# Four wait times of a hand-made schedule raised, and one barrier moved behind a projection, in a hybrid SSD and chunk-MLP encoder block

## Chip, cores and metric

The kernel runs on one core of a Trainium2 chip. The metric is the device time of one execution in microseconds, as the median of several. A core has a matrix engine (TensorE, PE in the rows; PEld are its weight loads), a vector engine (VectorE, DVE), a scalar engine (ScalarE, ACT), GpSimd (POOL), and SyncE (SP), which here issues nearly all DMA transfers. Each engine works through its own list of instructions in the order in which the program issued them, and waits there for semaphores.

## What is computed

One layer of a streaming encoder, for one prompt of 1024 rows and eight sample streams of 16 rows. Both go through the same weights, so the kernel treats them as nine tiles of 128 rows (tile 8 is the samples). In the reference, cut:

```python
h = rms_norm(x, norm_g[0]) * (1 + sc1) + sh1
z, xbc, dt_raw, uv = split(h @ w_in)
xbc_act = silu(causal_conv(xbc))              # 4 taps
dt = softplus(dt_raw + dt_bias)
y = ssd_scan(xs, dt, A, Bm, Cm, h0)           # chunked scan: gates, y_diag, y_off, state
y_ssd = rms_norm((y + d_skip * xh) * silu(z), ssd_norm_g)
u, v = split(gelu(uv)); v = layer_norm(v, v_ln_g, v_ln_b)
y_cmlp = u * (tril(w_s) @ v + b_s)
m = concatenate([y_ssd, y_cmlp]) @ w_out
x = x + g1 * rms_norm(m, norm_g[1])
h = rms_norm(x, norm_g[2]) * (1 + sc2) + sh2  # the second norm
x = x + g2 * rms_norm(square(relu(h @ w_ff1)) @ w_ff2, norm_g[3])
```

## The kernel before

The nine tiles are three groups of three (tiles 0 to 2, 3 to 5, 6 to 8). Every product is done in split fp32: an operand is a high part `hi` and a low part `lo`, and three matmuls hi·hi, hi·lo and lo·hi add up in one PSUM bank. ACT rounds the high part, DVE or GpSimd subtracts it to get the low part. Low parts of weights that a later group needs are stored to DRAM (`kl`) and loaded again (`wl<-kl`).

The program is written out by a scheduler of generators. A main generator issues the projections: `m_in(g)` for the input projection of group g (eight conv blocks `xbc`, z in two halves `pz0` and `pz1`, four `pu`, v in two halves `pv0` and `pv1`), then `m_out(g)` for the output projection (`wo`). After each block it yields an estimate of its time, and `tick` adds that to a build-time clock and steps eight lanes of side tasks. A side task issues a few instructions, yields a number from the table `WAIT` (`wait("dA", g)` takes `dA0`, `dA1`, `dA2` for the three groups), and is stepped again once the clock has passed that many ns. So the table decides behind how much projection work a side task's next matmul stands in the PE queue. Nothing of it is a wait on the chip. `finish(tasks)` ticks the clock in steps of 500 ns until the tasks are done, with no projection work issued meanwhile.

The side tasks that the change touches:

- `prep1_task(g)` makes `hT[g]`, the normed and modulated input of group g, transposed and split. Two rows of x give `ss`, GpSimd makes `r` from it, then comes `wait("prep1_tr", g)`. For each tile the matmul `pr` (L506) spreads `r`, DVE multiplies (L507), ACT modulates (L427; on DVE, L433 and L434, for tile 8), and a split writes `hT` (L238, L241). The first split of a group waits until the task given as `after` is done. For group 2 that is `ssd_tasks[1]`, since `hT[2]` lies in the memory of `gA[1]`, which that scan reads.
- `ssd_gates(g)` makes softplus on DVE (`ab`, `e` on ACT, `z`, `q`, `dt`, `dA`, L764 to L790), then `wait("dA", g)`, then the sums `pa` (L797, L798) on PE, the copy `nac` (L805) on DVE, `wait("pn", g)`, the transpose `pn` (L813), and from it `hl`, `lt` and `rr`.
- `ssd_tile(g, tl)` is the scan of a tile: `px`, `pbn` and `par` on PE, then `L` on ACT and DVE (L892), then `wait("yd", g)` and the products `yd`, `yo`, `su` on PE. All tiles of all groups run one after the other in lane A, and `tail_task` (z gate, norm, transposes `yT`) follows each in lane D.
- `prep2_first` makes the second norm of group 0, whose transposes `pt` (L252) wait for `M` (L456, L470). It runs behind `out_task(0)`.

`yT[2][0]` takes the memory of `M[0]`, so `ssd_task(2)` may begin only when `prep2_first` (`p0`) is done.

Of the kernel before, what the change touches and what calls it, by code (L numbers as in the profile page):

```python
# [41 lines left out]
def shape_constants():  # L42
# [14 lines left out]


WAIT = dict(
    L=12100, L0=3200, L1=0, L2=400, dA=28300, dA0=2400, dA1=2800, dA2=3200, evac=4100, gs1=4100, h0=4100, ln=5900,  # L60
    ln0=7300, ln1=9100, ln2=10000, lnr=5600, lnr0=2800, lnr1=600, lnr2=2000, modB=3000, modC=7600, mod_gate=2000,
    mod_load=8200, mod_mt=2100, next8=0, nexttile=6700, nexttile0=800, nexttile1=2400, nexttile2=1900, pn=20800,
    pn0=1900, pn1=0, pn2=3800, prep1_load=17400, prep1_load1=1700, prep1_load2=3200, prep1_next=13800,
    prep1_next1=4400, prep1_next2=1000, prep1_norm=11500, prep1_norm1=3300, prep1_norm2=800, prep1_split=40000,
    prep1_split1=400, prep1_split2=1000, prep1_stat=6500, prep1_stat1=1000, prep1_stat2=0, prep1_tr=5600,
    prep1_tr1=0, prep1_tr2=3500, prep2_load=1700, prep2_load0=200, prep2_load1=1500, prep2_load2=3600,
    prep2_next=3200, prep2_next0=2800, prep2_next1=2500, prep2_next2=5000, prep2_norm=6200, prep2_norm0=4000,
    prep2_norm1=3500, prep2_norm2=5000, prep2_split=1700, prep2_split0=1200, prep2_split1=800, prep2_split2=1500,
    prep2_stat=9600, prep2_stat0=1500, prep2_stat1=2500, prep2_stat2=4500, rr=11700, rr0=800, rr1=13000, rr2=400,
    set_load=10000, set_pcc=0, set_pw=2900, sp=13000, sp0=800, sp1=500, sp2=1900, sp_mid=22500, sp_mid0=9600,  # L70
    sp_mid1=0, sp_mid2=1400, sz=20900, sz0=1300, sz1=800, sz2=0, x1=14700, x10=2500, x11=7200, x12=4700, xr=29300,
    xr0=3000, xr1=2600, xr2=2700, yT=45700, yT0=2500, yT1=5600, yT2=2800, yc=23700, yc0=15400, yc1=16900,
    yc2=9500, yd=400, yd0=4500, yd1=6000, yd2=4900, yo8=2500, yr=11700, yr0=200, yr1=0, yr2=1100)
ENG = dict(p1hi=1, p2hi=0, ychi=0, yc=1, xdt=1, xw=1, xnD=1, L0=0, L1=0, sp=0, vg=0, vb=1, xr=1, S=0, rr=0, sz=1)
LO_POOL = {0, 1, 6, 7, 8, 9, 10, 11, 12, 13, 14, 15, 16, 17, 18, 19, 20, 21, 22, 24, 25, 26, 27, 28, 31, 32, 33, 35, 36, 39, 40, 41, 42, 43, 44, 46, 52, 53, 54, 55, 56, 60, 63, 64, 66, 68, 70, 72, 73, 77, 79, 80, 83, 85, 87, 89, 90, 91, 92, 93, 94, 95, 96, 97, 98, 100, 102, 103}
LOADS = [
# [41 lines left out]
def tile_block(ctx, tc, io, out):  # L118
# [59 lines left out]
    mod_tasks, out_tasks, flags = {}, {0: [], 1: [], 2: []}, {}  # L178
# [12 lines left out]
    def finish(*tasks):  # L191
        for t in tasks:
            while not t.done:
                tick(500.0)
# [382 lines left out]
    def m_proj_a(g, n, name, evac):  # L577
        accs = [None] * GT
        for half in range(2):
            wh, wl = w_next()  # L580
            for tl in range(GT):
                if half == 0:
                    accs[tl] = mmt(f"{name}_{tl}")
                xs = hT[g][half][:, :, :, P * tl:P * tl + P]
                o = accs[tl][:, 0:n]
                for k in range(4):
                    pe.matmul(o, xs[:, k, 0], wh[:, k, :], start=half == 0 and k == 0, stop=False)
                    pe.matmul(o, xs[:, k, 1], wh[:, k, :], start=False, stop=False)
                for k in range(4):
                    pe.matmul(o, xs[:, k, 0], wl[:, k, :], start=False, stop=half == 1 and k == 3)  # L590
                flush()
                if half == 1:
                    evac(tl, accs[tl])
                if tl == 0:
                    w_low()
                yield 4 * T_A
# [102 lines left out]
    def m_in(g, ct0=0):  # L699
# [8 lines left out]
        def ev_z(half):  # L708
            def f(tl, a):
                if half == 0:  # L710
                    dve.tensor_tensor(dtx[g][:, tl, :], a[:, 0:8], dtb, op=ALU.add)
                a = a[:, 8:264] if half == 0 else a[:, 0:256]
                th = gt(f"zt{g}{tl}{half}")
                act.activation(th, a, AF.Tanh, scale=0.5)
                dve.scalar_tensor_tensor(sz[g][:, tl, 256 * half:256 * half + 256], th, 1.0, a, op0=ALU.add, op1=ALU.mult)
                zdone[g] = tl + GT * half
            return f
# [2 lines left out]
            yield from m_proj_b(g, f"xbc{g}_{ct}", lambda a, ct=ct: xbc_evac(g, ct, a))  # L720
        if g > 0:
            finish(*gm_tasks[g - 1])
        if g == 2:
            finish(*out_tasks[0], p0)
        sz[g] = fslot(1 + g % 2, [P, GT, 512], F32, f"sz{g}")
        up[g] = fslot(0, [P, 4, GW], F32, f"up{g}")
        yield from m_proj_a(g, 264, f"pz0{g}", ev_z(0))
        ssd_tasks[g] = laneA.add(ssd_task(g))
        yield from m_proj_a(g, 256, f"pz1{g}", ev_z(1))
        for ct in range(4):  # L730
# [1085 lines left out]
```

## Time and profile before

| | |
|---|---|
| median of 3 runs | 1334.36 us (1334.32 to 1338.89) |
| profiled execution | 1334.28 us, span 1332.1 us, mean granted clock 0.976 |
| PE busy | 1254.1 us (94%) |
| PEld, DVE, ACT, GpSimd busy | 1115.8, 833.4, 629.6, 238.6 us |
| HBM traffic | 306 MB, 230 GB/s over the span |

The profile is one execution on the chip. A row of the order of time has its start, its length, engine, source line, operation, output and inputs, the count of instructions that it merges, and in brackets the idle time of the engine just before it with the instruction that ended it. Starts are microseconds from the span's start. The three groups' input and output projections fill the first 560 us or so; behind them come the MLP's products.

### The profile page before, as it was taken

How to read it: one execution, taken by the hardware profiler on the slowest of the kernel's cores; microseconds unless marked ns; L12 is line 12 of the kernel's file. 1: busy time of each engine (PE TensorE's matmuls, PEld its weight loads, DVE VectorE, ACT ScalarE, POOL GpSimd, SP SyncE). 2: the span in 40 equal slices, each digit the busy share in tenths (PEclk: the TensorE clock that was granted, in tenths of full speed). 3: DMA queues.
4: the chain of work that ended last, by engine and by line, in shares of the span. 5: the costliest groups of instructions: out<-in, count | busy, mean ns of one | idle time of the engine just before them, and what ended most of it. 6: DMA issues, size and time to landing. Idle time of an engine off the chain costs nothing. (4 is left out here: it accounts for less than half of the span.)

```text
span 1332.1 us, 18561 instructions
## 1 busy us (share of the span) xinstructions
PE 1254.1 (94%) x6815; PEld 1115.8 (84%) x6815; DVE 833.4 (63%) x1309; ACT 629.6 (47%) x1184; POOL 238.6 (18%) x266
## 2 busy tenths in 40 slices
PE   6988879989979999889999999999999999999996
PEld 4967767878779977789999999999988888888875
DVE  5476789566673543799885467576555335337666
ACT  3445534355574523546755444445433334344551
POOL 0133575147330443330000000000000000000001
PEclk9999979999999999989999999999999999999998
DMA  9778546745776467848448976665898337345863
GB/s 348 260 257 307 184 130 235 258 159 190 279 279 237 170 228 261 324 155 281 152 150 279 325 254 216 228 225 187 289 344 314 135 133 270 135 171 200 325 228 126
DMA packets 107154, 307.31 MB, mean 231 GB/s; under 512 B 12052, under 2 KB 31636, under 8 KB 107064
## 3 DMA queue, kind: packets, MB, share of 16 engines
q1 hardware_dynamic: 106632, 304.52, 64.6%
q10 hardware_dynamic: 432, 1.62, 0.3%
q8 instruction: 53, 0.87, 0.3%
q14 instruction: 37, 0.30, 0.1%
HBM read 232.47 MB, written 73.62 MB: 230 GB/s over the span
## 5 line engine op out<-in xcount | busy, mean ns | idle before, releaser
L241 DVE TENSOR_TENSOR bs<-br,bs 128x512 fp32r<-128x512 f32 x128 | 85.9, 689 | 107.2 <-ACT bs L238 106.9
L238 ACT CAST bs<-br 128x512 fp32r<-128x512 f32 x128 | 77.5, 619 | 146.5 <-PE G L1679 87.9
L1677 PE MATMUL P<-bs,as 128*128 128x512 f32 x336 | 132.1, 393 | 1.1 <-DVE acc L1740 1.1
L1679 PE MATMUL P<-bs,as 128*128 128x512 f32 x336 | 132.0, 393 | 0.0
L1678 PE MATMUL P<-bs,as 128*128 128x512 f32 x336 | 131.7, 392 | 0.0
L245 POOL TENSOR_SCALAR fr<-fss 128x1 f32<-128x1 f32 x9 | 2.8, 314 | 649.4 <-DVE fss L1637 649.4
L241 DVE TENSOR_TENSOR as<-ar,as 128x1536 fp32r<-128x1536 f32 x44 | 77.0, 1757 | 46.5 <-ACT as L238 46.5
L238 ACT CAST as<-ar 128x1536 fp32r<-128x1536 f32 x44 | 64.8, 1478 | 50.3 <-DMA ar<-fdA 26.2
L326 POOL TENSOR_TENSOR wl<-wr,wh 128x1024 fp32r<-128x1024 f32 (+1 forms) x28 | 70.3, 2514 | 86.7 <-ACT wh L319 52.1
L1677 PEld LDWEIGHTS P<-bs,as 128*128 128x128 f32 x336 | 63.1, 188 | 16.4 <-DVE acc L1740 2.0
L1678 PE MATMUL G<-bs,as 128*128 128x512 f32 x192 | 75.3, 392 | 0.0
L1677 PE MATMUL G<-bs,as 128*128 128x512 f32 x192 | 75.2, 392 | 0.0
L1679 PE MATMUL G<-bs,as 128*128 128x512 f32 x192 | 75.2, 392 | 0.0
L1679 PEld LDWEIGHTS P<-bs,as 128*128 128x128 f32 x336 | 63.1, 188 | 14.4
L1678 PEld LDWEIGHTS P<-bs,as 128*128 128x128 f32 x336 | 63.1, 188 | 14.2
L317 ACT CAST wh<-wr 128x1024 fp32r<-128x1024 f32 (+1 forms) x44 | 46.1, 1050 | 44.7 <-PE wo L1007 29.1
L652 DVE SCALAR_TENSOR_TENSOR cva<-pre,cwh,cva 128x256 f32<-128x256 f32 (+1 forms) x78 | 47.7, 653 | 12.4 <-ACT pre L634 11.5
L609 PE MATMUL xbc<-hT,wh 128*128 128x384 f32 x144 | 52.3, 363 | 0.0
L610 PE MATMUL xbc<-hT,wh 128*128 128x384 f32 x144 | 50.7, 352 | 0.0
L1447 DVE TENSOR_TENSOR wt<-wt 128x512 f32<-128x512 f32 x16 | 11.0, 689 | 51.6 <-DMA wt<-in_w_ff_dram 25.0
L1678 PEld LDWEIGHTS G<-bs,as 128*128 128x128 f32 x192 | 36.0, 188 | 8.2
L1677 PEld LDWEIGHTS G<-bs,as 128*128 128x128 f32 x192 | 36.0, 188 | 8.1
(938 smaller groups left out, 3674.0 us busy)
## 6 DMA issues: line engine op xcount, KB each, us to landing
wf<-in_w_f_dram SPq DMA_DIRECT2D x54, 512.0 KB, 4.8
wl<-kl SPq DMA_DIRECT2D x42, 512.0 KB, 4.2
wt<-in_w_ff_dram SPq DMA_DIRECT2D x16, 1024.0 KB, 6.3
td<-wt SPq DMA_DIRECT2D x64, 256.0 KB, 2.9
br<-in_w_ff_dram SPq DMA_DIRECT2D x32, 512.0 KB, 4.6
br<-td SPq DMA_DIRECT2D x32, 512.0 KB, 4.4
kl<-wl SPq DMA_DIRECT2D x26, 512.0 KB, 6.7
wr<-in_w_o_dram SPq DMA_DIRECT2D x24, 512.0 KB, 5.5
```

The lines of the kernel that those rows point to most:

```text
L238: act.copy(hi, src)
L241: dve.tensor_tensor(lo, src, hi.bitcast(F32), op=ALU.subtract)
L245: pool.tensor_scalar(r, ss, 1.0 / n, eps, op0=ALU.mult, op1=ALU.add)
L317: act.copy(hi, raw)
L326: (pool if i in LO_POOL else dve).tensor_tensor(lo, raw, hi.bitcast(F32), op=ALU.subtract)
L609: pe.matmul(o, wh[:, k, :], x[:, 0, :], start=k == 0, stop=False)
L610: pe.matmul(o, wh[:, k, :], x[:, 1, :], start=False, stop=False)
L652: dve.scalar_tensor_tensor(dst, tap, w(k), dst, op0=ALU.mult, op1=ALU.add)
L1447: dve.tensor_tensor(b11, b12, b11, op=ALU.subtract)
L1677: pe.matmul(bank, x[:, 0], b[:, 0], start=first, stop=False, skip_group_check=True)
L1678: pe.matmul(bank, x[:, 0], b[:, 1], start=False, stop=False, skip_group_check=True)
L1679: pe.matmul(bank, x[:, 1], b[:, 0], start=False, stop=last, skip_group_check=True)
```

## The change

Four numbers of the table go up: the ones ahead of `pr` in groups 1 and 2, ahead of `pa` in group 0, and ahead of `yd` in group 0. In `m_in(2)` the barrier on `out_tasks[0]` and `p0` moves from before the first half of z's projection to behind it, still ahead of `ssd_task(2)`. No instruction is added or taken away.

```diff
 WAIT = dict(
-    L=12100, ..., dA0=2400, dA1=2800, ...
+    L=12100, ..., dA0=6300, dA1=2800, ...
...
-    prep1_tr1=0, prep1_tr2=3500, ...
+    prep1_tr1=3000, prep1_tr2=6000, ...
...
-    yc2=9500, yd=400, yd0=4500, yd1=6000, ...
+    yc2=9500, yd=400, yd0=8500, yd1=6000, ...
@@ m_in
         if g > 0:
             finish(*gm_tasks[g - 1])
-        if g == 2:
-            finish(*out_tasks[0], p0)
         sz[g] = fslot(1 + g % 2, [P, GT, 512], F32, f"sz{g}")
         up[g] = fslot(0, [P, 4, GW], F32, f"up{g}")
         yield from m_proj_a(g, 264, f"pz0{g}", ev_z(0))
+        if g == 2:
+            finish(*out_tasks[0], p0)
         ssd_tasks[g] = laneA.add(ssd_task(g))
```

What that does to the order of instructions is to be seen at three places. The digits behind a name count within the kernel: `pa1` is pa of group 1, `pr7` is pr of tile 7, `xbc2_0` the first conv block of group 2; the number behind the last underscore only numbers the buffers.

The first place is DVE, from the last gelu step of group 0's v to the copy `nac` of group 0's gates. Before:

```order
L567 SCALAR_TENSOR_TENSOR gv102_1480<-gv102_1480,pv10_2_1398 128x256
L805 TENSOR_SCALAR nac40_1489<-pa0_1483 128x4x24
L808 TENSOR_TENSOR we0_1487<-nac40_1489,pa0_1483 128x24
L671 BN_STATS bst1_1496<-vt0_1220 128x6
L672 BN_AGGR bmv1_1497<-bst1_1496 128x2
L571 SCALAR_TENSOR_TENSOR vt0_1220<-gv102_1480,pv10_2_1398 128x256
```

And in the changed kernel, on the same engine:

```order
L567 SCALAR_TENSOR_TENSOR gv102_1480<-gv102_1480,pv10_2_1398 128x256
L671 BN_STATS bst1_1483<-vt0_1220 128x6
L672 BN_AGGR bmv1_1484<-bst1_1483 128x2
L571 SCALAR_TENSOR_TENSOR vt0_1220<-gv102_1480,pv10_2_1398 128x256
L677 TENSOR_SCALAR vt0_1220<-vt0_1220,bmv0_1460,lnr0_1463 128x512
L678 TENSOR_TENSOR vt0_1220<-vt0_1220,vg_117 128x512
L671 BN_STATS bst2_1517<-vt0_1220 128x6
L672 BN_AGGR bmv2_1518<-bst2_1517 128x2
L652 SCALAR_TENSOR_TENSOR cva1_0_1545<-pre1_0_1544,cwh_105,cva1_0_1545 128x384 x3
L805 TENSOR_SCALAR nac40_1559<-pa0_1553 128x4x24
```

`nac` moved behind seven operations of the gated MLP's norm and the three conv taps of the first conv block of group 1. On PE, `pa0` moved behind that whole block, and `pn0`, which reads `nac`, from the middle of the first block to the middle of the second.

The second place is PE around the gate sums of group 1. Before, they stand behind the first u block, and three more u blocks follow:

```order
L616 MATMUL pu1_0_2390<-hT10_1141,wl27_2251 128x384 x4
L616 MATMUL pu1_0_2390<-hT11_1142,wl27_2251 128x384 x4
L797 MATMUL pa1_2426<-dA1_2388,cs_81 128x24
L798 MATMUL pa1_2426<-dA1_2388,nones_93 128x24
L384 MATMUL pm25_2439<-modC0_1505,cT_97 32x512 x4
L609 MATMUL pu1_1_2447<-hT10_1141,wh28_2312 128x384
```

In the changed kernel, on PE:

```order
L616 MATMUL pu1_3_2487<-hT10_1141,wl30_2394 128x384 x4
L616 MATMUL pu1_3_2487<-hT11_1142,wl30_2394 128x384 x4
L797 MATMUL pa1_2550<-dA1_2548,cs_81 128x24
L798 MATMUL pa1_2550<-dA1_2548,nones_93 128x24
L384 MATMUL pm27_2563<-modC0_1492,cT_97 32x512 x4
L813 MATMUL pn1_2569<-cs_81,nac41_2556 128x128
```

`pa1` moved from behind the first u block to behind the fourth, and `pn1` follows with only a product of the modulation between. On DVE the softplus that makes `dA1` stands behind the gelu step that reads the fourth u block, in the changed kernel:

```order
L567 SCALAR_TENSOR_TENSOR gu13_2520<-gu13_2520,pu1_3_2487 128x384
L764 TENSOR_SCALAR ab1_2524<-dtx1_1496 128x24
L765 TENSOR_TENSOR ab1_2524<-ab1_2524,dtx1_1496 128x24
L777 TENSOR_SCALAR z1_2526<-e1_2525 128x24
L778 RECIPROCAL z1_2526<-z1_2526 128x24
```

Before, the same steps stood among those of the second half of z, ahead of the first u block.

The third place is PE at the end of group 0's output projection, where the last norm rows of group 2 stand. In the changed kernel (each L1009 row ends a block of six):

```order
L252 MATMUL yT5_3264<-cs_81,xn5_3039 128x128 x4
...
L1009 MATMUL wo010_3215<-wl41_3211,yTb0_1221 128x512 x2
...
L1009 MATMUL wo011_3224<-wl41_3211,yTb0_1221 128x512 x2
L506 MATMUL pr7_3299<-cs_81,r17_3021 128x128
...
L1009 MATMUL wo012_3231<-wl41_3211,yTb0_1221 128x512 x2
...
L506 MATMUL pr8_3350<-cs_81,r18_3063 128x128
...
L1009 MATMUL wo012_3231<-wl42_3241,yTb0_1221 128x512 x2
L609 MATMUL xbc2_0_3374<-hT20_3285,wh43_3273 128x384
```

Before, `yT5` stood in the first half of this projection, `pr7` 13 blocks of six and `pr8` ten ahead of `xbc2_0`; now it is four and one, with `yT5` six ahead. Of the second norm of group 0, `pt211`, `pt220` and `pt221` stood side by side ahead of z's first half of group 2; now three z blocks stand between `pt211` and `pt220`, and `pt220` and `pt221` end that half.

## Rows read from the trace of the kernel before

**Rows 1.** The page, part 1: busy us (share of span), instructions.

```profile
PE 1254.1 (94%) x6815; PEld 1115.8 (84%) x6815; DVE 833.4 (63%) x1309; ACT 629.6 (47%) x1184; POOL 238.6 (18%) x266
```

**Rows 2.** Waits of PE, whole span: us in total, times, longest.

```profile
PE yd L897 <- DVE L L892: 7.2, 6, 4.4
```

**Rows 3.** Order of time on PE, the five places that the change names.

```profile
94.14 0.49 PE L506 MATMUL pr<-cs,r 128*128 128x128 f32 x2 [2.92 <-POOL r L246]
...
145.26 0.37 PE L797 MATMUL pa<-dA,cs 128*128 128x24 f32 x2 [3.86 <-DVE dA L790]
...
172.61 3.33 PE L897 MATMUL yd<-xdt,L 128*128 128x64 f32 x16 [4.38 <-DVE L L892]
...
323.36 0.80 PE L506 MATMUL pr<-cs,r 128*128 128x128 f32 x2 [2.43 <-POOL r L246]
...
399.70 1.97 PE L252 MATMUL pt<-cs,M 128*128 128x128 f32 x8 [3.51 <-DVE M L470]
```

**Rows 4.** Windows: length, busy PE, PEld, DVE, ACT, POOL, PEclk, DMA, GB/s.

```profile
94.00:99.00 5.00, 4.86 (x21) 3.08 (x22) 2.31 (x5) 2.51 (x4) 2.43 (x6) 0.66 0.84 287
145.00:150.00 5.00, 4.74 (x20) 4.65 (x21) 3.73 (x12) 2.45 (x8) 1.43 (x5) 0.66 0.97 342
172.60:189.00 16.40, 13.52 (x57) 12.24 (x58) 11.86 (x13) 3.46 (x8) 10.63 (x9) 0.58 0.30 113
226.00:236.00 10.00, 9.54 (x45) 8.49 (x46) 9.05 (x13) 1.33 (x4) 7.66 (x4) 0.66 0.66 238
398.00:406.00 8.00, 6.30 (x32) 6.30 (x33) 2.20 (x6) 4.75 (x12) 0.00 (x0) 0.57 0.35 131
```

**Rows 5.** Windows inside group 2's conv blocks, and inside group 0's output projection.

```profile
350.50:361.50 11.00, 11.00 (x64) 10.96 (x64) 6.06 (x12) 7.15 (x17) 3.50 (x4) 1.00 0.81 285
343.00:350.00 7.00, 7.00 (x31) 5.66 (x31) 6.81 (x9) 1.89 (x3) 2.79 (x1) 1.00 0.69 218
```

**Rows 6.** Order of time on DVE, behind group 0's v projection.

```profile
146.82 0.41 DVE L567 SCALAR_TENSOR_TENSOR gv<-gv,pv 128x256 f32<-128x256 f32 x1
...
148.39 0.69 DVE L671 BATCH_NORM_STATS2 bst<-vt 128x6 f32<-128x512 f32 x1
...
158.73 2.43 DVE L652 SCALAR_TENSOR_TENSOR cva<-pre,cwh,cva 128x384 f32<-128x384 f32 x3
```

**Rows 7.** Window over the stage of group 1's first conv blocks.

```profile
155.00:189.00 34.00, 26.74 (x139) 24.02 (x138) 29.15 (x32) 10.44 (x20) 22.63 (x19) 0.80 0.30 99
```

**Rows 8.** Order of time on DVE: group 1's gates, and its last u gelu.

```profile
246.28 0.17 DVE L777 TENSOR_SCALAR z<-e 128x24 f32<-128x24 f32 x1
...
249.73 0.18 DVE L790 TENSOR_TENSOR dA<-dt,acol 128x24 f32<-128x24 f32 x1
...
268.25 0.56 DVE L567 SCALAR_TENSOR_TENSOR gu<-gu,pu 128x384 f32<-128x384 f32 x1 [1.47 <-ACT gu L566]
```

**Rows 9.** Window over the scan of tiles 3 and 4.

```profile
266.00:292.00 26.00, 22.75 (x158) 19.40 (x157) 18.31 (x26) 10.44 (x22) 11.09 (x12) 1.00 0.39 146
```

**Rows 10.** Order of time on DVE and ACT: hT of group 2.

```profile
331.20 3.37 DVE L241 TENSOR_TENSOR hT<-xT,hT 128x512 fp32r<-128x512 f32 x2 [0.45 <-ACT hT L238]
...
335.74 3.20 ACT L427 ACTIVATE xT<-xT,mod_sh,mod_G 128x128 f32<-128x128 f32 x8 [1.60 <-DVE xT L507]
...
345.00 1.65 DVE L433 TENSOR_TENSOR xT<-xT,mod_G 128x512 f32<-128x512 f32 x1
...
348.62 1.47 DVE L241 TENSOR_TENSOR hT<-xT,hT 128x512 fp32r<-128x512 f32 x2
```

**Rows 11.** Order of time on PE: a late low part in group 2's conv projection.

```profile
364.75 2.93 PE L616 MATMUL xbc<-hT,wl 128*128 128x384 f32 x8 [2.96 <-DMA wl<-kl]
```

**Rows 12.** Order of time on DVE: the pair ahead of yd, tiles 0 and 4.

```profile
170.94 2.97 DVE L892 TENSOR_TENSOR L<-L,bc 128x512 f32<-128x512 f32 x2
...
282.92 1.62 DVE L892 TENSOR_TENSOR L<-L,bc 128x512 f32<-128x512 f32 x2
```

**Rows 13.** Window over group 0's output projection.

```profile
308.30:350.40 42.10, 39.36 (x181) 31.93 (x180) 28.32 (x36) 25.20 (x51) 25.38 (x24) 0.96 0.59 206
```

More of the change, by code (lines that the diff above doesn't have):

```diff
@@ L59 @@
 WAIT = dict(
-    L=12100, L0=3200, L1=0, L2=400, dA=28300, dA0=2400, dA1=2800, dA2=3200, evac=4100, gs1=4100, h0=4100, ln=5900,
+    L=12100, L0=3200, L1=0, L2=400, dA=28300, dA0=6300, dA1=2800, dA2=3200, evac=4100, gs1=4100, h0=4100, ln=5900,
     ln0=7300, ln1=9100, ln2=10000, lnr=5600, lnr0=2800, lnr1=600, lnr2=2000, modB=3000, modC=7600, mod_gate=2000,
@@ L65 @@
     prep1_split1=400, prep1_split2=1000, prep1_stat=6500, prep1_stat1=1000, prep1_stat2=0, prep1_tr=5600,
-    prep1_tr1=0, prep1_tr2=3500, prep2_load=1700, prep2_load0=200, prep2_load1=1500, prep2_load2=3600,
+    prep1_tr1=3000, prep1_tr2=6000, prep2_load=1700, prep2_load0=200, prep2_load1=1500, prep2_load2=3600,
     prep2_next=3200, prep2_next0=2800, prep2_next1=2500, prep2_next2=5000, prep2_norm=6200, prep2_norm0=4000,
@@ L72 @@
     xr0=3000, xr1=2600, xr2=2700, yT=45700, yT0=2500, yT1=5600, yT2=2800, yc=23700, yc0=15400, yc1=16900,
-    yc2=9500, yd=400, yd0=4500, yd1=6000, yd2=4900, yo8=2500, yr=11700, yr0=200, yr1=0, yr2=1100)
+    yc2=9500, yd=400, yd0=8500, yd1=6000, yd2=4900, yo8=2500, yr=11700, yr0=200, yr1=0, yr2=1100)
 ENG = dict(p1hi=1, p2hi=0, ychi=0, yc=1, xdt=1, xw=1, xnD=1, L0=0, L1=0, sp=0, vg=0, vb=1, xr=1, S=0, rr=0, sz=1)
```

## Prediction

> **What bounds the kernel now.** I read the busy time per engine first, then the waits of the matrix engine, its order of time with the idle time ahead of each row, and the same stretches as windows with the granted clock. The matrix engine is busy for 1254.1 us, 94% of a span of 1332.1 us [rows 1], and works its queue in the order in which the program issued it. So the time is its work, plus the waits at small matmuls that stand in its queue before their inputs exist, plus what a lower clock costs behind such a wait. The list of waits shows the kind: the scan product yd waited 7.2 us in six places, 4.4 us in the longest [rows 2]. In order of time [rows 3], idle ahead of the row in brackets: the norm row pr at 94.14 (2.92) and 323.36 (2.43), the gate sums pa at 145.26 (3.86), yd at 172.61 (4.38), the transposes pt at 399.70 (3.51). These are the five places that the change names. Behind them the granted clock is at its lower level for a while, 1.2 instead of 2.4 GHz [rows 4]: a window of 5.00 us at a mean of 0.66 holds 5.00 x 0.34 x 2 = 3.4 us at half, which costs 1.7 us of busy time. That is so behind the first pr and behind pa, and I take it for the second pr too. Behind yd, 16.40 us at 0.58 hold 13.8 us at half; 16.40 - 13.52 = 2.9 us of it is idle, so half clock costs (13.8 - 2.9) / 2 = 5.4. From 226 to 236 it costs 3.4, from 398 to 406 (6.9 at half, some 1.3 of them idle) 2.8.
>
> **The change, term by term.** Against the profiled execution (1334.28 us, span 1332.1; the median of three runs is 1334.36, so nothing has to be converted). Two prices serve throughout [rows 5]: 64 matmuls of the conv projection take 11.00 us, 0.172 each, so a block of 24 is 4.1 us; 31 in the output projection take 7.00, so a block of six is 1.35.
>
> 1. pr of group 1 moves behind 16 more matmuls (2.8 us) and a product of the modulation that stood behind it; together that is more than the 2.92 that it waited. Gain up to 2.92 + 1.7 = 4.6. The stages behind it wait for low parts and for the Vector engine, which a matrix engine that comes earlier meets earlier, so I take -3.5, bounds -4.6 and 0.
>
> 2. pa of group 0 moves behind the whole first conv block. Its input is there by then: 3.86 + 1.7 gained. But the order of the Vector engine shows that the copy nac, which the transpose pn needs, now stands behind the three conv taps of that block and seven short operations. In before the gelu step ahead of them ends at 147.23; the seven take about 3.4 (at most 0.69 each), the taps 2.43 [rows 6], so nac comes at about 153. The matrix engine gets to pn at about 148.3: 145.26 - 3.86 = 141.4, the block 4.1, pa and eight matmuls some 2.0, and 0.7 as an estimate for the last rows of hT, which pa's wait hid. It waits 5 us there, with half clock behind. The wait moves: 0, bounds -4 and +3.
>
> 3. yd of tile 0 moves from 56 to 80 conv matmuls behind par, and from three small products of about 1 us to five: some 13 us become 19. Its factor L came 4.4 us after the 13, at 17. So the wait of 4.38 goes, and the 2.9 idle and 5.4 half clock behind it: 12.7. I take -12. The bound below comes from the Vector engine: from 155 to 189 it was busy 29.15 of 34.00 us [rows 7]; if all of that must still be done first, the stage gives 34.00 - 29.15 = 4.9. Bounds -5 and -13.
>
> 4. yd of tiles 1 and 2 moves as far. They waited 1.4 of the 2.8 that the other five have, and half clock from 226 costs 3.4. The scan's PSUM tiles follow more closely in one place, for which I leave 0.8: -4, bounds -5 and 0.
>
> 5. New wait. The scan of group 0 now ends eight z blocks and a u block later, and group 1's scan stands behind it in the same lane. So pa of group 1 moves from behind the first u block to right behind the fourth, the last, while its whole chain on the Vector engine stands behind that block's gelu step. From the end of the block: the gelu's 0.56 on the Vector engine and about as much on Scalar before it, some 0.6 for ab and the exponent, and from the first step of z to the end of dA 249.73 + 0.18 - 246.28, less about 0.4 for a foreign step, 3.2 [rows 8]. With the handovers 5.4 us, and nothing for the matrix engine in between. Then the transposes mt2 wait some 0.8 for the last modulation sum, and half clock costs 1.7 to 2.8: +8, bounds +5.4 and +9.5.
>
> 6. Group 1's scan waits from 266 to 292, 26.00 - 22.75 = 3.25 idle [rows 9], mostly go, since its products get five projection blocks between them: -2.5, bounds -3.3 and 0.
>
> 7. pr of group 2, tile 6, is five us of work later: -2.43 - 1.7 = -4, bounds -4.1 and -2.
>
> 8. New wait. hT of group 2 lies where group 1's scan reads gA, so its first split waits for that scan's end, which now falls into the output projection. Behind yT5 stand only six blocks of six and two pr, 8.7 us, before the conv projection of group 2 reads hT. The chain in before went from the split at 331.20 to 350.09, 18.9 us [rows 10]. Squeezed it is about 17 from yT5: 3.3 for yT's own split and tile 6's; 7.4 for tile 7 (the multiply 1.2, the modulation on Scalar 3.20, casts and split, copies of M between them); 6.3 for tile 8 (the multiply 1.2 once its load is there, then 350.09 - 345.00 = 5.1). So 17 - 8.7 = 8 us of wait, and half clock. I take +9.5, bounds +5 and +13.
>
> 9. The transfer that was late at 364.75 (2.96, half clock 1.7 more) [rows 11] gets those 8 us, and the loads of xr go behind it: -2.5, bounds -4.7 and 0.
>
> 10. Group 0's second norm: pt220 gets three z blocks (4.3 us) between itself and pt211; it was 3.51 late. -3.51 - 2.8, of which I take -5.5, bounds -6.3 and 0. The waits ahead of the earlier pt stay.
>
> Sum: -3.5 + 0 - 12 - 4 + 8 - 2.5 - 4 + 9.5 - 2.5 - 5.5 = -16.5, so 1334.3 - 16.5 = 1318.
>
> **A rule weighed.** The pair L892 that yd waits for took 2.97 us at 170.94, and 1.62 at 282.92 [rows 12]; GpSimd was busy 22.63 of the 34.00 us around the first [rows 7]. I read this as a collision that another order may avoid, and the sum counts it so. The Trainium skill, "SBUF — State Buffer", section "Who interferes with whom", says that a VectorE instruction with two SBUF inputs and a GpSimd instruction that reads SBUF hold one port pair in turn, the second blocked until the first is done. By that rule the order gains nothing as long as the same GpSimd work stands beside it, the Vector engine stays the bound of the stage, and the sum would be 1327 (the next rival's working). The rows bear the slowing out; whether the new order meets it as often, they can't show.
>
> **Rivals.** (a) Vector-bound stage: the 29.15 us stay ahead of the scan's second tile, term 3 is -5 and term 4 is -2: -16.5 + 7 + 2 = -7.5, 1327. For it: 86% busy there. Against it: the second tile's share, some 6 us, leaves the stage. This is where the rule of the Trainium skill above would end. (b) Slower: the Vector engine bounds both the stage that the scan leaves and the one that it enters. Two tiles of group 1 (about ten operations of 0.7 us each, 6.7 us a tile) fall into the output projection, where it was busy 28.32 of 42.10 us [rows 13]: 41.7 of 42.1. Terms 3, 4 and 6 are nothing (+18.5) and hT of group 2 comes 10 later: 1318 + 28.5 = 1346. It decides from the point where the Vector engine is over 95% busy in that stage. Against it: group 0's norm leaves the same stage. (c) The waits removed come back one for one within the stage, in terms 1, 7 and 10 (+13): 1331, no change. (d) The two new waits are half as long, since faster stages leave time to the loads and the splits: -8.7, 1309, and with full terms 3 and 4 1306.
>
> **How the numbers follow.** 1318: 0.50. (a) 0.18, half of it above and half below the limit of 0.5% (1327.6), which is about what a measurement of this kernel tells from no change. (b) 0.09. (c) 0.09. (d) 0.14. Faster 0.50 + 0.09 + 0.14 = 0.73 and a little of (c): 0.75; same 0.16; slower 0.09. The range 1306 to 1333 holds all but (b) and the outer parts of (c) and (d); the forecast's own is 1310 to 1326, which are the bounds of the terms added as independent errors.
>
> **What the profile after will show.** No idle time ahead of pr at tile 3 and 6; the first pa without wait but 4 to 6 us at pn; no wait at yd of group 0 and full clock around it; 5 to 6 us idle ahead of group 1's pa behind the last u block; 5 to 9 us idle where conv of group 2 starts; pt220 with under 1 us. From z of group 2 on, both traces should run alike. The prediction is wrong if the Vector engine is busy over 95% in the conv stage of group 1 or in the output projection of group 0, or if the matrix engine waits for weights' low parts that it now reaches earlier.

## The result, and the profile after

The changed kernel takes 1348.22 us (median of five runs) where the kernel before takes 1336.73 beside it: 0.9% slower, ratio 1.0091 with a 95% interval of 1.0069 to 1.0113. Forecast was 1318. The profiled execution took 1348.37 us, span 1346.6, mean granted clock 0.970. The page's busy times, against [rows 1]:

```profile
PE 1253.0 (93%) x6815; PEld 1114.9 (83%) x6815; DVE 839.5 (62%) x1309; ACT 630.2 (47%) x1184; POOL 238.4 (18%) x266
```

PE does the same work, so the loss is waiting. In the order of time of PE after the change (start, length, and in brackets the idle time ahead of the row and what ended it), the rows that stand where [rows 3] stood:

```profile
99.17 0.38 PE L506 MATMUL pr<-cs,r 128*128 128x128 f32 x2
104.66 3.10 PE L384 MATMUL pm<-modB,cT 128*32 128x512 f32 x8 [3.71 <-DMA modB<-in_w_mod_dram]
163.06 0.47 PE L813 MATMUL pn<-cs,nac 128*128 128x128 f32 x1 [7.06 <-DVE nac L805]
190.42 1.89 PE L897 MATMUL yd<-xdt,L 128*128 128x64 f32 x16
203.25 0.69 PE L866 MATMUL pbn<-cs,gA 128*128 128x128 f32 x2 [6.79 <-DVE modC L392]
276.91 0.59 PE L797 MATMUL pa<-dA,cs 128*128 128x24 f32 x2 [5.34 <-DVE dA L790]
370.60 0.69 PE L609 MATMUL xbc<-hT,wh 128*128 128x384 f32 x1 [8.76 <-ACT hT L238]
425.23 1.03 PE L252 MATMUL pt<-cs,M 128*128 128x128 f32 x8
```

Every wait that the change aimed at is gone: `pr` of group 1, `yd` of tile 0 and `pt` of tile 2 have nothing in brackets, nor have `pa` of group 0 and `pr` of tile 6, whose rows are not shown. Five others, of 3.71 to 8.76 us, stand elsewhere. Three were forecast: pn (5 us forecast, 7.06), pa of group 1 (5.4, 5.34), hT of group 2 (8, 8.76). Two were not: the modulation product behind `pr`, which now waits for its weight load, and `pbn`, which waits for a PSUM bank that the Vector engine still has to read (`modC`, L392, which stands behind six conv taps in its queue).

To find the stages, one thing must be known: up to 90 us the two programs are the same, yet the profiled executions differ by 4.1 us there, a difference between executions that other runs show too (last section). The profile of experiment e4 (the barrier alone) is a fair twin of before: the same program up to z of group 2, and it has that later start as well. It is no exact one: its output projection took 43.71 us where before's took 42.01, so a difference of under 2 us in one stage is not told apart here. Windows from the first conv block of group 1, cut where a projection begins (conv, z, u, v, output projection, conv of group 2); the columns are length; busy time of PE, PEld, DVE, ACT, POOL with counts; granted clock; DMA share; GB/s. The twin:

```profile
149.37:219.15 69.78, 57.96 (x327) 51.31 (x327) 59.96 (x76) 32.05 (x67) 43.29 (x40) 0.90 0.42 139
219.15:248.08 28.93, 25.30 (x194) 22.07 (x193) 22.48 (x34) 9.41 (x18) 15.08 (x13) 1.00 0.69 236
248.08:281.33 33.25, 30.46 (x180) 24.79 (x178) 19.23 (x41) 13.27 (x28) 5.81 (x6) 1.00 0.71 268
281.33:309.81 28.48, 27.57 (x213) 26.30 (x212) 20.16 (x35) 14.53 (x29) 15.57 (x13) 1.00 0.51 177
309.81:353.52 43.71, 39.42 (x180) 31.86 (x179) 30.23 (x37) 25.17 (x51) 25.18 (x24) 0.96 0.59 211
```

The changed kernel:

```profile
148.88:216.82 67.94, 51.80 (x295) 46.87 (x294) 59.91 (x76) 28.83 (x61) 42.26 (x38) 0.90 0.48 162
216.82:248.32 31.50, 27.71 (x202) 24.57 (x202) 23.91 (x33) 11.84 (x23) 13.81 (x11) 0.95 0.62 215
248.32:281.40 33.08, 27.32 (x159) 22.66 (x158) 15.09 (x40) 10.66 (x22) 3.33 (x6) 0.92 0.72 267
281.40:306.13 24.73, 24.73 (x195) 24.29 (x193) 17.28 (x27) 13.42 (x27) 9.11 (x8) 0.96 0.59 213
306.13:370.60 64.47, 49.55 (x248) 40.41 (x247) 41.29 (x59) 34.38 (x71) 38.09 (x38) 0.93 0.52 165
```

Scan products have moved from early windows into late ones, so the lengths can't be compared as they stand. Counting the products that stand behind each cut only after the change, at their lengths in the order of time (yd 1.89 us a tile, su 1.03, yo 1.08, px and yT 0.60, pbn 1.05, a par 0.48), 6.6 us of work are still missing at the start of z, 4.6 at u, 9.2 at v and 11.8 at the output projection; at conv of group 2 nothing is. With these added back the changed kernel is later than the twin by 4.3 us at z, 4.8 at u, 9.3 at v, 8.1 at the output projection, 17.1 at conv of group 2. From there to the end it is 5.7 us faster than before (976.0 against 981.7). 17.1 - 5.7 = 11.4, beside 11.5 between the medians; that they agree so closely is luck, since the twin itself stands 3.2 us behind before at conv of group 2. So it loses at three places: about 5 us where 19.5 should have been won, 4.5 at pa of group 1, and 9.0 in the output projection.

### The profile page after: what moved, and what is told of

Same layout as the page of the kernel before. It is cut to its first block, busy times and chain, and to the rows that moved or that the text cites. A ratio compares the mean times of both kernels' runs of the same rounds, so it can differ in the third digit from the quotient of the medians.

```text
span 1346.6 us, 18543 instructions
## 1 busy us (share of the span) xinstructions
PE 1253.0 (93%) x6815; PEld 1114.9 (83%) x6815; DVE 839.5 (62%) x1309; ACT 630.2 (47%) x1184; POOL 238.4 (18%) x266
## 5 line engine op out<-in xcount | busy, mean ns | idle before, releaser
L1677 PEld LDWEIGHTS P<-bs,as 128*128 128x128 f32 x336 | 63.1, 188 | 16.5 <-DVE acc L1740 2.0
L652 DVE SCALAR_TENSOR_TENSOR cva<-pre,cwh,cva 128x256 f32<-128x256 f32 (+1 forms) x78 | 57.6, 780 | 13.3 <-ACT pre L634 12.4
```

Of the source, the lines that this page charges most:

```text
L652: dve.scalar_tensor_tensor(dst, tap, w(k), dst, op0=ALU.mult, op1=ALU.add)
L1677: pe.matmul(bank, x[:, 0], b[:, 0], start=first, stop=False, skip_group_check=True)
```

## The experiments

The ratio is to runs of the kernel before on the same chip, with its 95% interval.

| | edit | median, us | ratio |
|---|---|---|---|
| e1 | norm rows later, alone | 1344.64 | 1.0069 (1.0046 to 1.0092) |
| e2 | gate sums later, alone | 1354.66 | 1.0139 (1.0111 to 1.0168) |
| e3 | scan products later, alone | 1358.51 | 1.0170 (1.0143 to 1.0197) |
| e4 | barrier alone | 1329.32 | 0.9952 (0.9933 to 0.9970) |
| e5 | gate sums and scan products | 1350.47 | 1.0113 (1.0087 to 1.0140) |
| e6 | changed, no low parts in conv of group 1 | 1335.14 | 0.9997 (0.9977 to 1.0018) |
| e7 | changed, group 1's yd earlier | 1350.20 | 1.0100 (1.0063 to 1.0137) |
| e8 | e1 and x^T of tile 8 in GpSimd's queue | 1330.94 | 0.9962 (0.9945 to 0.9979) |
| e9 | before, no low parts in conv of group 1 | 1325.61 | 0.9931 (0.9915 to 0.9947) |
| e10 | e8 and the barrier | 1327.56 | 0.9948 (0.9929 to 0.9968) |
| e11 | changed, those low parts on Vector | 1341.67 | 1.0059 (1.0042 to 1.0075) |
| e12 | changed, x^T of tile 8 in GpSimd's queue | 1348.50 | 1.0104 (1.0085 to 1.0123) |
| e13 | changed, gates of group 1 in a lane of their own | 1349.97 | 1.0088 (1.0056 to 1.0120) |
| e14 | e2 and x^T of tile 8 in GpSimd's queue | 1344.10 | 1.0048 (1.0024 to 1.0071) |
| e15 | e11 and e13 | 1341.62 | 1.0032 (1.0011 to 1.0053) |
| e16 | before, those low parts on Vector | 1331.42 | 0.9957 (0.9937 to 0.9977) |
| e17 | e10 and those low parts on Vector | 1322.49 | 0.9889 (0.9848 to 0.9930) |

**One part at a time.** Theory: the later scan products carry the loss. Rivals: every part loses a little, or the gates are the cause.

The edits are the hunks of the change's diff: e1 the two `prep1_tr` numbers, e2 `dA0`, e3 `yd0`, e4 the barrier.

```diff
-    prep1_tr1=0, prep1_tr2=3500, ...
+    prep1_tr1=3000, prep1_tr2=6000, ...
```

> The kernel before with the later norm rows of groups 1 and 2 alone (prep1_tr1 and prep1_tr2). Theory (the loss comes from issuing group 0's scan products later, and the other parts cost nothing): the wait of 2.9 us ahead of pr of group 1 goes, but the modulation product behind it now waits 3 to 4 us for its weight load, so that part gives 0; the wait of 2.4 us ahead of pr of group 2 goes with the half clock behind it, 0 to -4. Together -2 us, range -4 to +1. Rival 1 (every part loses a little, the sum is the 11.5 us measured): +3 us. Rival 2 (the loss sits in the late weight load of the modulation): +4 us, and the 3.7 us wait of the modulation product is there.

> The kernel before with the later gate sums of group 0 alone (dA0). Theory: pa's wait of 3.9 us goes and a wait of 5 to 7 us at the transpose pn takes its place, since the copy nac then stands behind the conv taps; yd of tile 0 keeps its distance to par and still waits 2 to 4 us; group 1's gate sums move by 6 us of products and hardly wait; +1 us, range -2 to +4. Rival 1 (every part loses a little): +3 us. Rival 2 (the gates are the cause, as every later wait hangs on them): +8 us or more, with a wait of over 3 us ahead of group 1's pa.

> The kernel before with the later first scan products of group 0 alone (yd0). Theory: this part carries the loss. The waits at yd of group 0 go (some 6 us), but the matrix engine meets the Vector engine's backlog further down in the same stage (a wait for a PSUM tile, 3 to 7 us); group 1's pa comes right behind the last u block and waits 5 us; hT of group 2 is late for the first conv block of group 2 by 5 to 8 us. Sum +8 us, range +5 to +13. Rival 1 (every part loses a little): +3 us. Rival 2 (the gates are the cause): 0 to -5 us, no wait at group 1's pa.

> The kernel before with the point moved up to which group 0's second norm must be issued (behind z's first half of group 2) alone. Theory: a gain by itself; the wait of 3.5 us ahead of the transposes of tile 2 goes with the half clock behind it: -5 us, range -3 to -6. Rival 1 (every part loses a little): +3 us. Rival 2 (the wait moves to the next thing that needs that norm or its slot, yT of group 2): 0 us, with a wait of 3 us within z of group 2 or at the start of its scan.

Only e4 came near its theory (6.4 us by its ratio, a little over the range). e2 came at the size of its second rival, but without the wait that was to go with it: pa of group 1 waited 1.8 us. e3 came far above its range, e1 above both its rivals. By their ratios the norm rows alone lose 9 us, the gates 19, the scan products 23; with the barrier's gain of 6 the parts sum to 44 us, while the whole change loses 12. So the parts don't add, and the theory that one part is the loss fell at once. What made e1 so dear was found in its queues. SyncE's queue of before, in order of time, and the row of GpSimd that waits for the store:

```profile
321.84 0.57 SPq L303 DMA_DIRECT2D wr<-in_w_o_dram  x1
334.60 0.33 SPq L491 DMA_DIRECT2D xT<-in_x_t_dram  x1
334.98 0.43 SPq L332 DMA_DIRECT2D kl<-wl  x1
...
340.28 2.40 POOL L326 TENSOR_TENSOR wl<-wr,wh 128x1024 fp32r<-128x1024 f32 x1 [6.26 <-DMA kl<-wl]
```

The same place of e1, with the row of DVE that frees the load's buffer and the row of GpSimd that waits for the store:

```profile
323.95 0.52 SPq L303 DMA_DIRECT2D wr<-in_w_o_dram  x1
337.52 0.33 SPq L491 DMA_DIRECT2D xT<-in_x_t_dram  x1
337.90 0.42 SPq L332 DMA_DIRECT2D kl<-wl  x1
...
335.22 2.28 DVE L241 TENSOR_TENSOR hT<-xT,hT 128x512 fp32r<-128x512 f32 x2 [5.57 <-ACT hT L238]
...
343.42 2.47 POOL L326 TENSOR_TENSOR wl<-wr,wh 128x1024 fp32r<-128x1024 f32 x1 [7.07 <-DMA kl<-wl]
```

The load of x^T of tile 8 needs the buffer of tile 6's x^T, which is free when tile 6's split ends: at 337.50 in e1, and 20 ns later the load is issued. Until then SyncE issued nothing for 13 us, though the store of low parts behind it had long been ready; GpSimd waits for that store (it frees the buffer of the next low part), and PE for GpSimd's low part. In before the queue stands nearly as long, 12.2 us, and PE waits 0.3 for the same. Counted from the start of the output projection (308.35 in before, 310.58 in e1), the load is issued after 26.3 and 26.9 us and the low part is ready after 34.3 and 35.3; but PE, which no longer waits at pr, is there to read it after 29.9 instead of 34.1. So the wait taken away at the norm row comes back at weights and stores that have nothing to do with it, mostly because PE is there sooner, less because the split is later. The test is to move that one load to another queue:

```diff
-            load(out=x, in_=x_t[GT * g + tl])
+            (pool.dma_start if GT * g + tl == 8 else load)(out=x, in_=x_t[GT * g + tl])
```

> The norm rows of groups 1 and 2 later as in the first experiment, and the load of x^T of tile 8 issued from GpSimd's queue instead of SyncE's. Theory (that load waits in SyncE's queue for its buffer, until the split of tile 6 ends, and holds up the stores of low parts and the weight loads behind it; a later norm row makes that longer; that is where the 8.6 us of the first experiment came from): the wait of 5.5 us for the low part in the output projection and the waits of 4.8 us for loads of low parts in the conv projection of group 2 fall to under 3 together; in all -5 to -9 us against the first experiment, 1336 to 1340. Rival (the loss comes from the Scalar engine's queue or from the hT chain, the stores are late for other reasons): 1343 to 1346 with those waits in place.

> The kernel before with the later gate sums of group 0 (as in the second experiment, +18.6 us) and the load of x^T of tile 8 in GpSimd's queue. Theory (what the gate part costs alone beyond the pair comes from SyncE's queue: it was held for 12.2 us by the load of x^T of tile 6 or 7 and again until 350.7 by that of tile 8, and the output projection waited 8.6 us for low parts): the second low part's wait of 5.0 goes, -5 to -9 us against the second experiment, 1346 to 1350. Rival (the loss sits in the waits at pn, 6.6, and behind the scan): 1352 to 1356.

> The changed kernel with the load of x^T of tile 8 issued from GpSimd's queue. Theory (in the changed kernel that load stands later in SyncE's queue, where it held it for 3 us only, and hT of group 2 waits for the scan of group 1): the wait ahead of the first conv block of group 2 stays at 7 to 9, the time within -3 and +1 us of the changed kernel. Rival (SyncE's queue is behind the changed kernel's loss as well): -8 us or more.

The wait of PE for low parts in the output projection, in e1 and then in e8:

```profile
PE wo L1009 <- POOL wl L326: 5.5, 1, 5.5
```

```profile
PE wo L1009 <- POOL wl L326: 1.0, 2, 0.9
```

e8 is 1.1% faster than e1, more than its theory's range, and 0.4% faster even than before: the theory of the queue holds. How much of the 0.4% the moved load would give by itself is not known, since before with that load alone moved was not run. e14 takes 0.9% off the gate part in the same way, a little more than its range, and leaves 0.5%. For e3 it was not tried, and its trace has no wait for low parts in the output projection; what makes it so dear alone stays open. In the whole change tile 8's load is not the cause: e12 is level with it, as expected. There hT of group 2 waits for other things.

That does not clear the queue itself. One group earlier the load of x^T of tile 5 stands behind the split of tile 3 in the same way. SyncE and below it DVE, in the twin:

```profile
117.84 0.33 SPq L491 DMA_DIRECT2D xT<-in_x_t_dram  x1
...
116.52 1.29 DVE L241 TENSOR_TENSOR hT<-xT,hT 128x512 fp32r<-128x512 f32 x2
```

In the changed kernel SyncE, DVE, GpSimd and PE:

```profile
121.44 0.33 SPq L491 DMA_DIRECT2D xT<-in_x_t_dram  x1
...
117.93 3.49 DVE L241 TENSOR_TENSOR hT<-xT,hT 128x512 fp32r<-128x512 f32 x2
...
118.21 2.65 POOL L326 TENSOR_TENSOR wl<-wr,wh 128x1024 fp32r<-128x1024 f32 x1 [2.70 <-DMA wr<-in_w_a_dram]
...
135.33 2.34 POOL L326 TENSOR_TENSOR wl<-wr,wh 128x1024 fp32r<-128x1024 f32 x1 [5.64 <-DMA kl<-wl]
...
137.72 1.22 PE L590 MATMUL pv<-wl,hT 128*128 128x256 f32 x4 [3.30 <-POOL wl L326]
```

Both traces begin u of group 0 at nearly the same time (93.62 and 93.73). The split of tile 3 now falls beside a subtraction of GpSimd, the load is 3.6 us later, the stores behind it too, and PE waits 4.4 us for low parts in v of group 0 where the twin waits 2.1. The profiled execution of e7 runs the same program up to there, but its modulation product waited 2.7 us instead of 3.7; its split took 1.28 us, its low parts 1.7 us of wait, and the stretch from u to conv 51.37 us instead of 55.15. No run moves tile 5's load, so what it costs the whole change is not measured.

**The pair.**

> The kernel before with the later gate sums and the later first scan products of group 0 together, without the later norm rows and the moved barrier. Alone they cost 18.6 and 22.4 us. Theory (both push the same scan, and its lateness is paid once, at hT of group 2 and at group 1's pa): 1353 to 1359 us, +17 to +23; since the whole change stands at +11.5 and its barrier part gains 6.8, this pair should stand at about +18 and the norm rows add nothing beside it. Rival (the two costs add, they are different waits): 1372 us or more, +36 to +41.

At +15 us the pair costs less than either part alone, a little under the range; the costs don't add. Its waits are those of the whole change (pn 7.1, pbn 6.8, pa 5.3, hT 8.8), to the tenth.

**Why nothing came of terms 3 and 4.** In the conv stage of group 1 the Vector engine is busy for 59.9 us before and after, with less scan work after. Its conv taps of that stage (min/median/max in ns), before, and then after:

```profile
L652 DVE SCALAR_TENSOR_TENSOR cva<-pre,cwh,cva x21: 606/620/1669, 158.7 to 215.0; 128x384 f32<-128x384 f32 x21
```

```profile
L652 DVE SCALAR_TENSOR_TENSOR cva<-pre,cwh,cva x21: 610/1398/2781, 158.0 to 214.6; 128x384 f32<-128x384 f32 x21
```

And the order of time after, DVE and below it GpSimd, around the longest:

```profile
190.42 6.38 DVE L652 SCALAR_TENSOR_TENSOR cva<-pre,cwh,cva 128x384 f32<-128x384 f32 x3
...
189.33 2.69 POOL L326 TENSOR_TENSOR wl<-wr,wh 128x1024 fp32r<-128x1024 f32 x1
191.98 1.59 POOL L693 TENSOR_TENSOR vt<-vt,up 128x512 f32<-128x512 f32 x1
...
193.99 2.39 POOL L326 TENSOR_TENSOR wl<-wr,wh 128x1024 fp32r<-128x1024 f32 x1
```

Three taps take 6.38 us there, 3 x 0.62 alone. The first and the last of them by themselves:

```profile
190.42 2.02 DVE L652 SCALAR_TENSOR_TENSOR cva<-pre,cwh,cva 128x384 f32<-128x384 f32 x1
...
194.02 2.78 DVE L652 SCALAR_TENSOR_TENSOR cva<-pre,cwh,cva 128x384 f32<-128x384 f32 x1
```

The subtractions end at 192.02 and 196.38, these taps at 192.43 and 196.80, each 0.4 us later: a tap beside a subtraction ends only when the subtraction has. The edits: first the eight subtractions of that stage are left out (the low parts are set to zero), in the changed kernel and in before; then they are done by the Vector engine instead.

```diff
+                if 15 <= i < 23:
+                    pool.memset(lo.bitcast(F32), 0.0)
+                    continue
...
-LO_POOL = {..., 14, 15, 16, 17, 18, 19, 20, 21, 22, 24, ...}
+LO_POOL = {..., 14, 24, ...}
```

> The changed kernel in which the low parts of the eight weight blocks of group 1's conv projection are set to zero by GpSimd (which reads nothing for it) instead of subtracted; left out are eight subtractions of 2.4 us, and the result is without these low parts. Theory (GpSimd's subtractions hold up the Vector engine's conv taps in this stage, which is why removing the wait at yd gained so little): the taps, 4.0 to 6.4 us for three beside a subtraction, go back to 2.0 to 3 us; the waits at pn (7.1) and at the PSUM tile of pbn (6.8) fall to under 6 together; the stage from the first conv block of group 1 to z of group 1, 67.9 us, falls to 58 to 63; in all -5 to -10 us against the changed kernel. Rival 1 (the Vector engine's own work of some 60 us bounds the stage whatever GpSimd does): the stage keeps 66 to 68 us and the taps their length. Rival 2 (the stage gets shorter but the later waits at pa of group 1 and at hT of group 2 eat it): stage 58 to 63, in all -2 to 0 us.

> Control for the experiment without low parts: the kernel before, with the low parts of the same eight weight blocks of group 1's conv projection set to zero instead of subtracted (eight subtractions left out, the result is without them). Theory (GpSimd's subtractions slow the Vector engine in this stage in both kernels, and the waits at yd are their symptom, so shifting products against each other only moves the waits): the stage from the first conv block to z of group 1, 71.2 us, falls to 57 to 64, the wait at yd of tile 0 from 4.4 to under 1, in all -6 to -12 us against before. Rival (only the changed order runs into the subtractions; the gain of 13 us found there is what the change added): the stage stays at 68 to 71 and the time within 3 us of before.

> The changed kernel with the low parts of the eight weight blocks of group 1's conv projection subtracted by the Vector engine instead of GpSimd (nothing left out). Theory (what counts is that the two hold each other up, not the amount of work): the median conv tap of that stage falls from 1.40 us to 0.62 to 0.8, which gives the Vector engine 21 x 0.7 = 15 us for 8 x 1.2 = 10 us of added subtractions; the stage falls from 67.9 to 62 to 66 us and the time by 2 to 6 us against the changed kernel. Rival (the Vector engine's queue is the bound, more work in it is more time): the stage grows to 70 to 76, +2 to +8 us.

> The kernel before with the low parts of group 1's conv projection on the Vector engine (nothing left out): the control of the same edit on the changed kernel, where it gave 6.5 us. Theory (the changed order runs into the collisions more: 13.4 us of the Vector engine's time there against 5.6 here, by the runs without low parts): the added 9.8 us of subtractions are not paid back, stage from the first conv block to z of group 1 68 to 73 us, time -3 to +3 us against before. Rival (the collisions are a cost of the kernel, as large in the order before): stage 62 to 66, -5 to -8 us.

The stage without the subtractions, in before (e9) and in the changed kernel (e6); 71.17 and 67.94 us were the lengths with them:

```profile
142.72:206.09 63.37, 57.21 (x328) 51.30 (x327) 54.38 (x78) 31.74 (x67) 33.10 (x40) 0.92 0.46 158
```

```profile
145.50:197.38 51.88, 49.17 (x296) 44.77 (x295) 46.55 (x66) 27.36 (x57) 29.77 (x37) 0.97 0.59 201
```

The Vector engine's busy time falls by 5.6 us in before and by 13.4 in the changed kernel, the stage by 7.8 and by 16.1, and the median tap is 0.62 us in both. So the collisions are there in both orders, and the changed order meets more of them. The changed stage lacks 6.6 us of scan products and has 0.4 of pa in addition; with the 6.2 us added it is 3.0 us longer than before's with the subtractions, 5.3 us shorter without them. The change would have won some 5 us there, and collisions took some 8. e6 came beyond its theory in both, 13 us and this stage. One expectation of e9 failed: yd of tile 0 still waits 3.2 us, so its wait is not only the subtractions' doing. On the Vector engine the stage takes 58.88 us in the changed kernel (e11) and 65.81 in before (e16), again with taps of 0.62.

Two cautions. Over the whole program the edit gives about the same in both kernels (0.9% and 0.7% left out, 0.3% and 0.4% on the Vector engine, intervals that overlap), so the rival of e16 was right: it is mainly a cost of the kernel. And without the subtractions the change still loses 0.7%, so the stage's failure to gain is not the loss. The output projection without them, in before (e9) and in the changed kernel (e6):

```profile
298.64:340.56 41.92, 39.34 (x180) 31.85 (x178) 28.23 (x36) 25.11 (x51) 25.52 (x24) 0.96 0.61 208
```

```profile
288.88:353.09 64.21, 50.89 (x248) 41.72 (x246) 42.61 (x59) 34.37 (x71) 38.12 (x38) 0.91 0.50 165
```

Of the 22.3 us between them 11.8 are products moved there; the other 10.5 are lost as they were with the subtractions (9.0), and they take up what the conv stage had won.

**Where the loss is.** That leaves group 1's gates and scan.

e7 issues its first scan products earlier; e13 puts `gates_front`, which is `ssd_gates` as far as dA, in a lane that is empty then, and `ssd_gates(1)` waits for it at build time.

```diff
-    yc2=9500, yd=400, yd0=8500, yd1=6000, ...
+    yc2=9500, yd=400, yd0=8500, yd1=3000, ...
```

```diff
         ssd_tasks[g] = laneA.add(ssd_task(g))
+        if g == 1:
+            gd_of[g] = {}
+            fronts[g] = laneE.add(gates_front(g, gd_of[g]))
```

> The changed kernel with group 1's first scan products issued earlier (yd1 3000 instead of 6000), so that group 1's scan ends about 2.5 us of products earlier within the output projection and frees the slot in which hT of group 2 lies. Theory (the loss in the output projection is the wait for that scan's end): the wait of 8.8 us ahead of the first conv block of group 2 falls to 4 to 7, new waits at yd of group 1 of 0 to 2; in all -2 to -5 us against the changed kernel. Rival (the chain of the norm from split to split on Scalar and the loads of x^T bound it, not the scan): the wait stays at 8 to 9 us and the time within 1 us.

> The changed kernel with the chain of group 1's gates (from dt to dA, some 20 short operations of the Vector engine) issued in a lane of its own, during z and u of group 1, instead of behind the scan of group 0 in the same lane. Theory (pa of group 1 waits because that chain stands behind the last u block): the wait of 5.3 us at pa of group 1 goes, the whole scan of group 1 comes 1.3 us of products earlier, the wait ahead of the first conv block of group 2 stays at 7 to 9 since the matrix engine comes earlier too; in all -4 to -7 us against the changed kernel. Rival (the time is regained before the output projection, which waits for loads or for the Vector engine anyway): the wait goes and the time stays within 2 us.

> The changed kernel with the low parts of group 1's conv projection on the Vector engine (-6.5 us alone) and group 1's gates in a lane of their own. Theory (two separate causes): the gains add, 1335 to 1338 us, -10 to -13 against the changed kernel, level with the kernel before. Rival (the slower stage covered the gates' wait): 1340 to 1343.

The waits of e7 that matter (us in total, times, longest):

```profile
PE wo L1006 <- ACT mj L1012: 5.4, 1, 5.4
PE xbc L609 <- ACT hT L238: 3.9, 1, 3.9
PE yd L897 <- POOL xdt L887: 3.3, 1, 3.3
```

And of e13, in which pa of group 1 waits no more:

```profile
PE yT L252 <- DVE xn L865: 4.8, 2, 2.9
PE mt L252 <- DVE modC L392: 4.7, 1, 4.7
PE xbc L609 <- ACT hT L238: 3.7, 1, 3.7
```

Both edits do what they should and neither wins anything. In e7 the wait at hT falls from 8.8 to 3.9, and 5.4 for a PSUM bank behind Scalar's copies and 3.3 at yd come in its place. In e13 the 5.3 us at pa go, and the transposes right behind it wait 4.7 for the modulation's last sum, which pa's wait had covered (0.4 in the changed kernel); hT's wait halves too, and yT takes it up. So my theory of two waits that could be taken away one by one fell: the stretch from group 1's gates to conv of group 2 is a chain of several waits of like length. e15 came at its rival; it stands at 1.0032 beside 1.0059 for e11, and whether the gates' lane adds something there these runs don't tell.

**A version that beats both.**

> The parts of the change that gain, together: later norm rows, the moved barrier, and the load of x^T of tile 8 in GpSimd's queue; gate sums and scan products of group 0 as before. Theory (the gains are of different waits, 5.1 us for the first and third together, 6.8 for the barrier): 1322 to 1326 us, ratio to before 0.990 to 0.993. Rival (the two gains overlap, both bring the second norm of group 0 earlier): 1328 to 1331.

> The version with later norm rows, moved barrier and GpSimd's queue, and the low parts of group 1's conv projection on the Vector engine. Theory: as for the kernel before, -3 to +3 us against that version's 1327.6. Rival: -5 to -8 us, 1320 to 1323.

e10 came at the edge of its rival. Its 0.9948 is level with the 0.9952 of the barrier alone, so of e8's gain nothing is seen beside the barrier. e17 (later norm rows, moved barrier, that load in GpSimd's queue, those low parts on the Vector engine, gates and scan products as before) takes 1322.49 us, 1.1% less than before. Against e10 that is 5 us by the medians and 8 by the ratios, the rival's size or a little more; the two intervals touch, so the size is not settled.

## Why the prediction was wrong, step by step

The step that failed is term 3, and with it its neighbours: **terms 1 to 4** were to give 19.5 us and cost 4.8, which is 24 of the 28 us between the forecast difference (-16.5) and the measured one (+11.5). The sum took PE's waits as gained where they were removed; the Vector engine and the low parts behind them were as late as before or later, and PE met them a few products on. That the change loses against before is another matter: terms 5 to 8, the new waits, were forecast and came, and e6 against e9 shows the loss also where the Vector engine is relieved.

- Term 1 (-3.5): +3.6 in the profiled execution. The wait at pr went; the product behind it came earlier and waited 3.7 us for its weights, which the forecast had not named, and v of group 0 waited 4.4 us for low parts instead of 2.1, which it had. From the start of u the changed kernel is at conv of group 1 after 55.15 us, the twin, without pa's wait, after 51.57. Executions differ here: beside the 51.92 us of e5, whose norm rows stand as in before, the later norm rows took 51.37 in e7 and 54.60 in e12. The gain of 3.5 came in none.
- Term 2 (0): right in kind. pa's 3.9 us went, pn waited 7.06 where 5 was forecast, since the taps ahead of `nac` took 4.07 us beside a subtraction instead of 2.43 and `nac` then waited 0.72 for GpSimd.
- Terms 3 and 4 (-16): with term 2 +1.2. yd's waits went, and 6.8 us came at pbn, with 2.2 at par in the stage behind. The sum took the bound at which the collision of [rows 12] is avoided. The rows of the order of time show the opposite: the median tap is 2.3 times as long. The bound of -5 that term 3 carried, or the 5 us of e6 against e9, is about what the order itself is worth. So of the 17 us between -16 and +1.2 some 8 are collisions, and the rest is gain that the order does not have even without them.
- Terms 5 and 6 (+5.5): +3.3. The wait at pa of group 1 is 5.34 against 5.4.
- Terms 7 and 8 (+5.5): +9.0. The wait at hT is 8.76 against 8, and pr of tile 6 waits no more; but four smaller ones in the output projection (2.38 at the first block, 1.61 at par, 1.18 at yT, 0.59 for a low part: 5.8 us) were not in the sum.
- Terms 9 and 10 (-8): -5.7. No row for the late load is left, and pt of tile 2 has no wait; pt of tile 0 and 1 wait 4.00 and 1.74 where the forecast let them stay. The barrier alone gives 0.48%, 6.4 us, against the 5.5 of term 10. From z of group 2 to the end the two traces take 930.8 and 930.6 us, alike as forecast.

Rival (a), the Vector-bound stage, named the place and stopped at 1327, since it kept the gain of terms 1 and 4. Rival (b), 1346, came nearest in time, but its condition was not met: the Vector engine was busy for 59.91 of 67.94 us in the conv stage and 41.29 of 64.47 in the output projection, 88% and 64%, not 95%. On the rule weighed there (the Trainium skill, "SBUF — State Buffer", "Who interferes with whom"), that the second of two such instructions is blocked until the first is done: the trace agrees, for a tap, which reads two SBUF tiles, ends 0.4 us after the subtraction beside it, and three take 6.38 us instead of 1.86. The sum that followed the rule, 1327, was nearer than 1318. Two sums of the forecast are off by themselves, without bearing on this: its terms' bounds, added as independent errors, reach 1330 and not 1326, and rival (d) with full terms 3 and 4 comes to 1307.

Of its signs of being wrong the forecast had one right: PE waits longer for low parts, in v of group 0, though there because they come later. What stays open is which of the waits in the output projection would have to go, and in which order, for the changed kernel to get its 9 us back there; each of the two tried alone was replaced by the next.

## What to carry to other kernels

In a queue worked in order, look at what stands behind a waiting entry, not only at the entry: with a load that waits for its buffer in the queue that issues nearly all DMAs, an edit lost 9 us; with that one load in another engine's queue, edit and move together gained 5. When a wait is removed, ask whether the engine that released it was late for a reason that stays; here it was slowed by GpSimd, and PE met it again a few products on. Parts of a change to such a schedule don't add up: 44 us one by one were 12 together, so a part has to be tried in the order in which it is to run.

## What the runs showed of the hardware

The same program does not start alike in every execution. Windows from 10 to 30 us, where every kernel here issues the same instructions, of before:

```profile
10.00:20.00 10.00, 6.57 (x43) 4.75 (x41) 6.21 (x15) 6.82 (x15) 1.48 (x4) 1.00 1.03 410
20.00:30.00 10.00, 9.35 (x85) 6.90 (x85) 8.66 (x18) 2.64 (x4) 0.00 (x0) 1.00 0.99 384
```

and of the changed kernel:

```profile
10.00:20.00 10.00, 6.32 (x42) 4.56 (x40) 6.02 (x15) 6.62 (x15) 1.48 (x4) 0.83 1.03 411
20.00:30.00 10.00, 9.31 (x51) 6.31 (x52) 6.63 (x13) 1.40 (x3) 0.00 (x0) 0.52 0.76 283
```

After the same 6.3 to 6.6 us of matrix work in the window from 10 to 20, the granted clock stays at 1.00 (2.4 GHz) in one execution and falls to 0.52 (nearly all at 1.2 GHz) in the other, which is then 4 us later at 90 us. There are starts between these: e6 has 0.72 and 0.60. Part of the spread between runs of one kernel may come from it, which no run here separates. The delay does not stay as it is: the twin is 4.0 us late at 94 us, 1.5 at the output projection and 3.2 at conv of group 2.
